# Attention on one core: the products of probabilities and values written as rows, instead of as columns that are copied and turned back

## The chip, the cores and the metric

The kernel runs on one core of a Trainium2 chip. TensorE (PE in the profile, PEld for its weight loads) does the matrix products, VectorE (DVE), ScalarE (ACT) and GpSimd (POOL) the rest; SyncE (SP) issues most transfers. The metric is the device time of one execution in microseconds (us), and less is better.

## What is computed

Two request groups, a prompt of 1024 tokens and a sample of 256, pass through two layers. Each layer has a mixer (an HGRN2 recurrence with 5 heads beside an attention with 6 heads in 3 groups) and a mixture of 16 experts. The change lies in the attention:

```python
def dilated_window_attention(q, k, v, dilation, radius):
    ...
    s = jnp.einsum('bnqhd,bnkhd->bnhqk', qs, kw)
    s = jnp.where(valid[None, :, None], s, -jnp.inf)
    m = jnp.max(s, axis=-1, keepdims=True)
    p = jnp.exp(s - m)
    l = jnp.sum(p, axis=-1, keepdims=True)
    o = jnp.einsum('bnqhk,bnkhd->bnqhd', p, vw) / jnp.transpose(l, (0, 1, 3, 2, 4))
    lse = jnp.transpose((m + jnp.log(l))[..., 0], (0, 1, 3, 2))
```

Windows and dilations are (128, 1), (512, 4) and (2048, 16), with two heads of 64 columns in each group. All of it is in fp32.

## The kernel before

Each layer runs in two parts. `mixers` holds the projections, the HGRN scan, the attention and the output projection; `moe` holds the experts. Within `mixers` the work is written as generators. `lanes` takes turns among them: each yields the number of nanoseconds that its next step should wait, and a clock that `mm`, `tr` and the wrapped engines advance by a modelled cost decides who records its next instructions. So the order of the instructions on each engine is fixed when the program is built, and a changed number of products or of yields in one generator moves the steps of the others as well.

The attention of a layer is cut into units of 128 queries and one head group (two heads): 24 units for the prompt and 6 for the sample, 60 over the two layers. A unit has one or two blocks of at most 128 keys; over both layers there are 96 blocks, so 192 products of probabilities and values (one for each block and head). Four of the units, at the two ends of the prompt in each layer, have one block of 64 keys. Up to three units are in flight, beside the HGRN lanes.

A unit's steps in `attention` are: load the rows; turn keys and queries (`kT`, `qT`); scores into PSUM (`sc`); mask and maximum on VectorE; exponentials on ScalarE; turn the probabilities (TensorE into a `tp` tile, ScalarE copies them to `PT`); multiply them with the values into another `tp` tile, `po`; bring the result to `ao` as rows (queries on partitions), and store it. `tp` is a PSUM pool of two buffers that the HGRN steps and the output projection share. `qT` is a pool of three buffers in SBUF, and before the change the copied result `oT` takes a buffer of it too: rows of the profile named `qT<-tp` are turned queries and copied results together, and TensorE rows `tp<-ident,qT` are the turns back.

In the profile a TensorE row such as `tp<-PT,kv 128*64 128x128` reads: written tile, moving operand, stationary operand; rows times columns of the stationary operand; shape of the moving operand. Each fp32 product leaves two records, one for each of its two passes with a weight load of its own; the products of fp32r operands (`mm<-hTh,wH` and the like, 512 columns wide) and the turns leave one. `lv<-Q,km 128*32` are small products of the HGRN scan, 32 columns and 32 rows of the array each, 16 in a group. Lines of helpers are L182 (`mm`), L196 (`tr`) and L111 (every operation of VectorE and ScalarE).

Of the kernel before, what the change touches and what calls it, by code (L numbers as in the profile page):

```python
# [8 lines left out]
F32 = mybir.dt.float32  # L9
# [3 lines left out]
AF = mybir.ActivationFunctionType  # L13
# [5 lines left out]
P = 128  # L19
# [106 lines left out]
class Body:  # L126
# [722 lines left out]
    def attention(self, groups, pool, width, scan):  # L849
        nc, I, sc_ps, tp = self.nc, self.I, self.scp, self.tpp  # L850
        am = pool.tile([P, 640], F32, name="am")
        nc.sync.dma_start(am, I["c_amask"])

        def rows_dma(g, dst, w0, nw, gi, spec):

            start, dims = spec
            base = g.qkv
            nsub = dims[0][1] if len(dims) == 2 else 1
            inner = dims[-1]
            for s in range(nsub):  # L860
                s0 = start + (s * dims[0][0] if len(dims) == 2 else 0)
                src = bass.AP(tensor=base.tensor, offset=base.offset + s0 * 9 * P + (3 * w0 + gi) * P,
                              ap=[[inner[0] * 9 * P, inner[1]], [3 * P, nw], [1, P]])
                nc.sync.dma_start(dst[s * inner[1]:(s + 1) * inner[1]], src)

        def transposed(src, name, bufs):
            n = src.shape[0]
            t = tp.tile([P, P], F32, name="tp")
            self.tr(t[:, :n], src)
            o = pool.tile([P, P], F32, name=name, bufs=bufs)  # L870
            nc.scalar.activation(o[:, :n], t[:, :n], AF.Copy)
            return o

        tiles = {}

        def unit(g, gi, qspec, kspec, m0):
            if kspec == "same":
                r = pool.tile([P, 3, P], F32, name="qkvr", bufs=3)
                rows_dma(g, r, 0, 3, gi, qspec)
                keys = [dict(n=P, k=r[:, 1], v=r[:, 2])]  # L880
            else:
                r = pool.tile([P, 1, P], F32, name="qr", bufs=3)
                rows_dma(g, r, 0, 1, gi, qspec)
                keys = []
                for name, k0, stride, n in kspec:
                    if name not in tiles:
                        kv = pool.tile([P, 2, P], F32, name="kv", bufs=5)
                        rows_dma(g, kv[:n], 1, 2, gi, (k0, [[stride, n]]))
                        tiles[name] = dict(n=n, k=kv[:n, 0], v=kv[:n, 1])
                    keys.append(tiles[name])  # L890
            yield 2500.0
            for k in keys:
                if "kT" not in k:
                    k["kT"] = transposed(k["k"], "kT", 5)
            qT = transposed(r[:, 0], "qT", 3)
            yield 150.0
            W = sum(k["n"] for k in keys)
            cuts, c = [], 0
            for k in keys:
                cuts.append((c, k["n"], k))  # L900
                c += k["n"]
            ps = [sc_ps.tile([P, W], F32, name="sc") for _ in range(2)]
            for c, n, k in cuts:
                for hd in range(2):
                    s = slice(64 * hd, 64 * hd + 64)
                    self.mm(ps[hd][:, c:c + n], qT[s, :], k["kT"][s, :n], start=True, stop=True)
            sc = pool.tile([P, 2, W], F32, name="sc", bufs=3)
            o = pool.tile([P, 132], F32, name="ao", bufs=3)
            nm = self.sm.tile([P, 2], F32, name="nm")
            for hd in range(2):  # L910
                nc.vector.tensor_tensor_reduce(sc[:, hd], ps[hd], am[:, m0:m0 + W], op0=OP.add, op1=OP.max,
                                               scale=1.0, scalar=NEG, accum_out=o[:, 128 + hd:129 + hd])
            nc.vector.tensor_scalar(nm, o[:, 128:130], -1.0, None, op0=OP.mult)
            self.after_all()
            for hd in range(2):
                nc.scalar.activation(sc[:, hd], sc[:, hd], AF.Exp, bias=nm[:, hd:hd + 1],
                                     accum_out=o[:, 130 + hd:131 + hd])
            yield 150.0
            pt = tp.tile([P, 2, len(keys), P], F32, name="tp")
            PT = pool.tile([P, 2, len(keys), P], F32, name="PT", bufs=3)  # L920
            for hd in range(2):
                for j, (c, n, k) in enumerate(cuts):
                    self.tr(pt[:n, hd, j], sc[:, hd, c:c + n])
            if all(n == P for c, n, k in cuts):
                nc.scalar.activation(PT, pt, AF.Copy)
            else:
                for j, (c, n, k) in enumerate(cuts):
                    nc.scalar.activation(PT[:n, :, j], pt[:n, :, j], AF.Copy)
            yield 150.0
            po = tp.tile([P, P], F32, name="tp")  # L930
            for j, (c, n, k) in enumerate(cuts):
                for hd in range(2):
                    s = slice(64 * hd, 64 * hd + 64)
                    self.mm(po[s], k["v"][:, s], PT[:n, hd, j], start=j == 0, stop=j == len(keys) - 1)
            oT = pool.tile([P, P], F32, name="qT", bufs=3)
            nc.scalar.activation(oT, po, AF.Copy)
            yield 150.0
            po = tp.tile([P, P], F32, name="tp")
            self.tr(po, oT)
            nc.vector.tensor_copy(o[:, 0:P], po)  # L940
            start, dims = qspec
            nsub = dims[0][1] if len(dims) == 2 else 1
            inner = dims[-1]
            for s in range(nsub):
                s0 = start + (s * dims[0][0] if len(dims) == 2 else 0)
                dst = bass.AP(tensor=g.ob.tensor, offset=g.ob.offset + (gi * g.nt + s0) * 132,
                              ap=[[inner[0] * 132, inner[1]], [1, 132]])
                nc.sync.dma_start(dst, o[s * inner[1]:(s + 1) * inner[1]])

        units = [(g,) + t for g in groups for t in self.attn_units(g)]  # L950

        def paced(i, u):
            yield from self.until(scan, "first", min(10, int(i * 0.4)))
            yield from unit(*u)
            scan[u[0].name] += 1

        tasks = [lambda i=i, u=u: paced(i, u) for i, u in enumerate(units)]
        yield from self.lanes(tasks, width)
# [509 lines left out]
```

## Time and profile before

| what | value |
| --- | --- |
| median of 3 runs | 3365.02 us (3363.21 to 3366.41) |
| the profiled execution | 3368.75 us, its span 3367.0 us |
| PE busy | 3251.8 us, 97% of the span, 23718 instructions |
| PEld busy | 2469.6 us, 73% |
| DVE busy | 2118.5 us, 63% |
| ACT busy | 1727.9 us, 51% |
| granted TensorE clock, mean | 0.984 |

The span runs from the first to the last instruction of the profiled execution; its own time has 1.75 us around that. Busy shares are averages over stages with different limits. The attention units stand from 365 to 726 us (layer 1) and from 2048 to 2407 us (layer 2), beside the HGRN scan and the first tiles of the output projection.

### The profile page before, as it was taken

To read this page: it belongs to the slowest core of one execution; us is meant where nothing else is said; L and a number is where in the kernel's file an instruction comes from. 1 tells how busy PE (TensorE), PEld (TensorE's weight loads), DVE (VectorE), ACT (ScalarE), POOL (GpSimd) and SP (SyncE) were. 2 spreads that over 40 slices of the span, in tenths; PEclk is the share of its full clock that TensorE was granted. 3 is DMA by queue.
4 is the path that set the end of the run, shared out by engine and by line. 5 is a ranking of instruction groups with operands and counts; after the bars stand their busy time and mean duration, and the time that the engine had idled before them with its cause. 6 is when DMAs were issued, how large, how long until landed. Compare 5 with 4: busy or idle time off the path is not lost.

```text
span 3367.0 us, 58960 instructions
## 1 busy us (share of the span) xinstructions
PE 3251.8 (97%) x23718; PEld 2469.6 (73%) x23718; DVE 2118.5 (63%) x4205; ACT 1727.9 (51%) x2509; POOL 248.9 (7%) x215
## 2 busy tenths in 40 slices
PE   8999999989799999999999999999997999999997
PEld 8999877767566666666699997777674666666664
DVE  6461377774756676666665615787746766676666
ACT  5331465552456666566553315555433666666665
POOL 0000000000011111011100000000000111111001
PEclk9999999999899999999999999999998999999999
DMA  5341221243498889888753412212434988889887
GB/s 186 109 134 51 87 63 52 75 136 124 162 319 284 285 284 332 287 280 283 240 167 99 129 52 83 62 57 76 139 126 158 330 314 285 284 288 327 284 283 282
DMA packets 421185, 639.52 MB, mean 190 GB/s; under 512 B 31024, under 2 KB 189360, under 8 KB 420912
## 3 DMA queue, kind: packets, MB, share of 16 engines
q1 hardware_dynamic: 396240, 556.83, 47.5%
q0 software_dynamic: 23952, 76.30, 8.3%
q8 instruction: 187, 3.06, 0.4%
q10 hardware_dynamic: 720, 2.62, 0.3%
q14 instruction: 86, 0.70, 0.1%
HBM read 550.09 MB, written 85.58 MB: 189 GB/s over the span
## 4 chain that ended last, share of the span: by engine, by line
PE 42%; DVE 3%; DMA 3%; ACT 1%; issue 1%; SPq 0%; DVEq 0%; ACTq 0%
PE mm L182 21%; PE lv L182 11%; PE sc L182 6%; PE tp L196 3%; PE tp L182 2%; DMA raw<-in_w_up_dram 1%; DVE wL L111 1%; DMA raw<-in_w_in_dram 0%; ACT wH L111 0%; DVE ind L111 0%; DVE val L111 0%; DMA obr<-obp 0%; DMA sg<-vgp 0%; DVE raw L111 0%; DMA xbp<-ye,idxp 0%
## 5 line engine op out<-in xcount | busy, mean ns | idle before, releaser
L111 DVE TENSOR_TENSOR wL<-raw,wH 128x2048 fp32r<-128x2048 f32 (+2 forms) x448 | 960.1, 2161 | 394.7 <-ACT wH L111 393.3
L111 ACT ACTIVATE wH<-raw 128x2048 fp32r<-128x2048 f32 (+2 forms) x448 | 812.4, 1816 | 255.2 <-PE lv L182 110.3
L182 PE MATMUL mm<-wH,hTh 128*128 128x320 f32 (+1 forms) x1120 | 367.0, 328 | 4.6 <-ACT wH L111 4.6
L182 PE MATMUL mm<-wL,hTh 128*128 128x320 f32 (+1 forms) x1120 | 360.6, 322 | 1.2 <-DVE wL L111 1.2
L182 PE MATMUL mm<-wH,hTl 128*128 128x320 f32 (+1 forms) x1120 | 360.8, 322 | 0.0
L182 PE MATMUL sc<-raw,xs 128*32 128x512 f32 x2048 | 231.0, 599 | 0.0
L182 PEld LDWEIGHTS mm<-wH,hTh 128*128 128x128 f32 x1120 | 211.8, 189 | 7.1 <-ACT wH L111 5.1
L182 PE MATMUL mm<-wH,xh 128*128 128x512 f32 x512 | 205.5, 401 | 8.9 <-ACT xh L111 8.9
L182 PEld LDWEIGHTS mm<-wL,hTh 128*128 128x128 f32 x1120 | 212.0, 189 | 2.2 <-DVE wL L111 1.9
L182 PEld LDWEIGHTS mm<-wH,hTl 128*128 128x128 f32 x1120 | 211.7, 189 | 0.7 <-DVE hTl L111 0.3
L182 PE MATMUL mm<-wL,xh 128*128 128x512 f32 x512 | 205.6, 402 | 3.6 <-DVE wL L111 3.6
L182 PE MATMUL lv<-wL,xh 128*128 128x512 f32 x512 | 200.6, 392 | 3.5 <-DVE wL L111 3.5
L182 PE MATMUL mm<-hTh,wH 128*128 128x512 f32 x480 | 202.8, 423 | 0.0
L182 PE MATMUL mm<-wH,xl 128*128 128x512 f32 x512 | 201.8, 394 | 0.0
L182 PE MATMUL lv<-wH,xl 128*128 128x512 f32 x512 | 200.2, 391 | 0.0
L182 PE MATMUL lv<-wH,xh 128*128 128x512 f32 x512 | 200.1, 391 | 0.0
L182 PE MATMUL mm<-hTl,wH 128*128 128x512 f32 x480 | 195.8, 408 | 0.0
L182 PE MATMUL mm<-hTh,wL 128*128 128x512 f32 x480 | 194.0, 404 | 0.0
L1317 POOL DMA_INDIRECT xbs<-yS,sidx x62 | 95.3, 1537 | 1111.7 <-ACT yS L111 980.3
L182 PEld LDWEIGHTS sc<-raw,xs 128*32 128x32 f32 x2048 | 63.9, 111 | 148.2 <-issue 146.0
L182 PE MATMUL sc<-raw,hs 128*32 128x512 f32 x1024 | 150.6, 598 | 0.0
L111 DVE TENSOR_TENSOR K<-K,TT 128x256 f32<-128x256 f32 (+1 forms) x360 | 123.9, 374 | 39.1 <-PE lv L182 27.9
(305 smaller groups left out, 6315.2 us busy)
## 6 DMA issues: line engine op xcount, KB each, us to landing
raw<-in_w_up_dram SPq DMA_DIRECT2D x128, 1024.0 KB, 15.7
raw<-in_w_down_dram SPq DMA_DIRECT2D x128, 1024.0 KB, 8.9
raw<-in_w_gate_dram SPq DMA_DIRECT2D x126, 1024.0 KB, 14.0
raw<-in_w_in_dram SPq DMA_DIRECT2D x36, 512.0 KB, 4.2
wr<-in_w_in_dram SPq DMA_DIRECT2D x24, 512.0 KB, 3.8
raw<-in_w_in_dram SPq DMA_DIRECT2D x16, 640.0 KB, 4.6
vgp<-vgo SPq DMA_DIRECT2D x64, 160.0 KB, 1.8
raw<-in_w_in_dram SPq DMA_DIRECT2D x12, 768.0 KB, 4.7
```

Source lines behind the costliest of these rows:

```text
L111: return fn(out, *args, **kw)
L182: self.last_mm = self.nc.tensor.matmul(out, lhsT, rhs, start=start, stop=stop)
L196: ins = self.nc.tensor.transpose(out, src, self.ident[:k, :k])
L1317: nc.gpsimd.indirect_dma_start(out=xs2, out_offset=at, in_=yS[64 * h:64 * h + 64], in_offset=None, compute_op=OP.add)
```

## The change

The product of probabilities and values changes its roles. Before, the values are stationary (128 keys by 64 columns of one head) and the turned probabilities move (128 queries); the result has the head's columns on partitions, the two heads on the two halves of the partitions. ScalarE copies it, TensorE turns it, and VectorE copies it to `ao`. After, the turned probabilities are stationary (128 keys by 128 queries) and the head's 64 value columns move; the result has queries on partitions already, and VectorE copies it to `ao` at once. The copy, one wait of the generator (`yield 150.0`), one `tp` tile and the turn fall away. The loop over heads now stands outside the loop over key blocks.

```diff
             po = tp.tile([P, P], F32, name="tp")
-            for j, (c, n, k) in enumerate(cuts):
-                for hd in range(2):
-                    s = slice(64 * hd, 64 * hd + 64)
-                    self.mm(po[s], k["v"][:, s], PT[:n, hd, j], start=j == 0, stop=j == len(keys) - 1)
-            oT = pool.tile([P, P], F32, name="qT", bufs=3)
-            nc.scalar.activation(oT, po, AF.Copy)
-            yield 150.0
-            po = tp.tile([P, P], F32, name="tp")
-            self.tr(po, oT)
+            for hd in range(2):
+                s = slice(64 * hd, 64 * hd + 64)
+                for j, (c, n, k) in enumerate(cuts):
+                    self.mm(po[:, s], PT[:n, hd, j], k["v"][:, s], start=j == 0, stop=j == len(keys) - 1)
             nc.vector.tensor_copy(o[:, 0:P], po)
```

How the order moves is shown at three places. The first is on TensorE in layer 1, beside the level products of an HGRN unit (`lv<-Q,km`), where three attention units end close together; a row here is one product, written tile, moving and stationary operand, shape of the output.

```order
-L182 MATMUL tp<-PT,kv 64x128 x8
-L196 MATMUL tp<-ident,qT 128x128
-L182 MATMUL lv<-Q,km 32x32 x8
-L196 MATMUL tp<-ident,qT 128x128
-L182 MATMUL lv<-Q,km 32x32 x3
-L196 MATMUL tp<-ident,qT 128x128
-L182 MATMUL lv<-Q,km 32x32 x5
+L182 MATMUL tp<-kv,PT 128x64 x4
+L182 MATMUL mm<-hTh,wH 128x512
+L182 MATMUL mm<-hTl,wH 128x512
+L182 MATMUL mm<-hTh,wL 128x512
+L182 MATMUL mm<-hTh,wH 128x512
+L182 MATMUL tp<-kv,PT 128x64 x4
+L182 MATMUL mm<-hTl,wH 128x512
+L182 MATMUL mm<-hTh,wL 128x512
+L182 MATMUL lv<-Q,km 32x32 x16
```

Three turns that cut the group of 16 small products into pieces are gone, and the units' products now stand among the 512-column products, apart from each other.

The second place is further on in layer 1, on TensorE, where a pair of units stands among the projection's products only.

```order
 L182 MATMUL mm<-hTh,wH 128x512
-L182 MATMUL tp<-PT,kv 64x128 x8
-L196 MATMUL tp<-ident,qT 128x128
-L182 MATMUL mm<-hTl,wH 128x512
-L182 MATMUL mm<-hTh,wL 128x512
-L196 MATMUL tp<-ident,qT 128x128
+L182 MATMUL tp<-kv,PT 128x64 x8
+L182 MATMUL mm<-hTl,wH 128x512
+L182 MATMUL mm<-hTh,wL 128x512
 L182 MATMUL mm<-hTh,wH 128x512
 L182 MATMUL mm<-hTl,wH 128x512
```

The eight products stand at the same place in either order; the two turns behind them fall away, and nothing takes their place.

The third is on VectorE, early in layer 1: the copies into `ao` among the steps of an HGRN level (`K`, `Q`, `ac`).

```order
+L111 COPY ao<-tp 128x128
 L111 COPY_PREDICATED ac<-cmask,lv 128x128
 L111 TENSOR_TENSOR Q<-Q,TT 128x32x2x8
+L111 COPY ao<-tp 128x128
 L111 TENSOR_TENSOR qk<-qk,mm 128x512
-L111 TENSOR_TENSOR K<-K,TT 128x16x16 x2
-L111 COPY ao<-tp 128x128 x3
+L111 TENSOR_TENSOR K<-K,TT 128x16x16
+L111 COPY ao<-tp 128x128
+L111 TENSOR_TENSOR K<-K,TT 128x16x16
```

Three copies that stood together behind a level's steps now stand one by one, two of them ahead of that level's steps.

## Rows read from the trace of the kernel before

**Rows 1.** Busy time of each engine in two stretches (us, instructions).
```profile
core 0: us, PE busy (x) PEld busy (x) DVE busy (x) ACT busy (x) POOL busy (x), PEclk, DMA share, GB/s
360.00:660.00 300.00, 298.29 (x3433) 229.16 (x3433) 208.25 (x633) 173.91 (x389) 4.52 (x6) 1.00 0.23 67
...
2300.00:2405.00 105.00, 98.10 (x1068) 73.75 (x1068) 82.95 (x289) 62.68 (x154) 3.49 (x5) 0.93 0.31 90
```

**Rows 2.** The tile PT: TensorE records, duration ns min/median/max, first and last start, forms.
```profile
L182 PE MATMUL tp<-PT,kv x288: 269/273/476, 378.9 to 2377.9; 128*64 128x128 f32 x136, 64*64 64x128 f32 x8
...
L182 PE MATMUL tp<-PT,qkvr x96: 272/273/473, 568.0 to 2397.8; 128*64 128x128 f32 x96
```

**Rows 3.** The tile qT, the same view.
```profile
L111 ACT ACTIVATE qT<-tp x120: 258/277/297, 371.1 to 2398.2; 128x128 f32<-128x128 f32 x120
...
L196 PE MATMUL tp<-ident,qT x60: 270/327/421, 381.7 to 2399.6; 128*128 128x128 f32 x60
```

**Rows 4.** TensorE's timeline: start us, us, merged records; sixteen records in one group.
```profile
501.91 1.09 PE L182 MATMUL tp<-PT,kv 128*64 128x128 f32 x16
```

**Rows 5.** TensorE's timeline, weight loads, around the router's products on 16 columns.
```profile
783.14 0.30 PEld L182 LDWEIGHTS sc<-quad,xT 128*128 128x128 f32 x2
...
783.36 0.19 PEld L182 LDWEIGHTS mm<-oL,wH 128*128 128x128 f32 x1
```

**Rows 6.** TensorE's timeline: HGRN products with 128 stationary columns, back to back.
```profile
2404.85 0.39 PE L182 MATMUL tp<-v,A 128*128 128x128 f32 x2
2405.07 0.61 PE L182 MATMUL tp<-S,Q 128*128 128x128 f32 x4
2405.52 0.39 PE L182 MATMUL tp<-v,A 128*128 128x128 f32 x2
```

**Rows 7.** Timelines of TensorE's products and of its weight loads: a score on 64 moving columns.
```profile
371.41 0.43 PE L182 MATMUL sc<-kT,qT 64*128 64x64 f32 x2
...
371.41 0.29 PEld L182 LDWEIGHTS sc<-kT,qT 64*128 64x128 f32 x2 [0.39 <-ACT qT L111]
```

**Rows 8.** TensorE's timeline: a turn back among 512-column products.
```profile
381.26 0.39 PE L182 MATMUL mm<-hTh,wL 128*128 128x512 f32 x1
381.49 0.39 PE L182 MATMUL mm<-hTh,wH 128*128 128x512 f32 x1
381.72 0.27 PE L196 MATMUL tp<-ident,qT 128*128 128x128 f32 x1
381.75 0.47 PE L182 MATMUL mm<-hTl,wH 128*128 128x512 f32 x1
382.06 0.39 PE L182 MATMUL mm<-hTh,wL 128*128 128x512 f32 x1
```

**Rows 9.** TensorE's timeline: turns back among the small products.
```profile
435.40 0.33 PE L196 MATMUL tp<-ident,qT 128*128 128x128 f32 x1
435.66 0.26 PE L182 MATMUL lv<-Q,km 128*32 128x32 f32 x6
435.85 0.33 PE L196 MATMUL tp<-ident,qT 128*128 128x128 f32 x1
436.11 0.31 PE L182 MATMUL lv<-Q,km 128*32 128x32 f32 x10
```

**Rows 10.** TensorE's timeline: a unit's eight records among 512-column products.
```profile
537.14 0.40 PE L182 MATMUL mm<-hTh,wL 128*128 128x512 f32 x1
537.47 0.66 PE L182 MATMUL tp<-PT,kv 128*64 128x128 f32 x8
538.06 0.50 PE L182 MATMUL mm<-hTh,wH 128*128 128x512 f32 x1
```

**Rows 11.** TensorE's waits: us in total, times, longest.
```profile
PEld tp L196 <- ACT qT L111: 4.1, 18, 0.3
```

**Rows 12.** The tile ao: VectorE's copies, and the engine's idle time ahead of them (us, times).
```profile
L111 DVE COPY ao<-tp x60: 278/291/292, 382.0 to 2400.0; 128x128 f32<-128x128 f32 x60
...
  PE tp L196: 35.2, 44
```

**Rows 13.** Busy times, as in Rows 1, near the end of layer 2's scan.
```profile
2357.00:2367.00 10.00, 8.61 (x130) 7.11 (x131) 8.82 (x22) 7.76 (x15) 0.00 (x0) 0.66 0.41 122
```

## Prediction

> **What bounds the kernel.** I read the busy times by stretch first, because the attention stands in two stretches only. In the 300 us of layer 1 in which most units run, TensorE is busy for 298.3 us at full clock, VectorE for 208 and ScalarE for 174 [rows 1]. So in that stretch TensorE's own occupation is the time, and a step of another engine costs nothing unless TensorE waits for it. Only the seams behind the scans are different: in the 105 us from 2300 us TensorE idles for 6.9 us and its mean granted clock is 0.93 [rows 1]. The rest of the reading is therefore a count of TensorE's occupation: how many passes, how many turns, and what it costs to change how the array is divided.
>
> Durations in the timeline overlap (a record of 0.27 us is followed by the next after 0.11), so I price by the distance from one start or end to the next, never by durations.
>
> **The passes.** The tile PT has 288 and 96 records, 384 in all [rows 2]: 192 products, two passes each. Before, the two heads of a block run side by side on the two halves of the array's columns. The group of sixteen records lasts 1.09 us; without its last record's 0.273 us [rows 2] it is 0.82 us for seven steps of two records each, 0.117, in which the first weight load still counts [rows 4]. I take 0.11 for a step of both heads: 384 / 2 x 0.11 = 21.1 us before.
>
> After, the stationary operand has 128 columns and takes the whole array, so the heads follow one another: 384 steps. No row shows a whole-array fp32 product with 64 moving columns, so I bound it. Fp32 products with 128 stationary and 128 moving columns run at (2405.52 - 2404.85) / 6 = 0.112 us a pass [rows 6]. Halving the moving columns helps only if the weight load keeps up. With 16 moving columns, two loads take 0.30 us where one takes 0.19, so they start 0.11 apart, and the next load starts at 0.22 [rows 5]: the load of 128 fp32 columns is the limit, whatever moves. The score on 64 moving columns agrees: its second load ends 0.29 after the first starts, again 0.11 apart [rows 7]. So 0.11 a pass: 384 x 0.11 = 42.2 us, **21.1 us more** than before. The lower bound is what the 64 columns need when weights cost nothing: the second record of that score starts 0.43 - 0.27 = 0.16 after the first, and 0.16 - 0.106 = 0.054 is left for moving [rows 7]; 384 x 0.054 = 20.7, 0.4 less than before. The upper bound is that load and move add up, 0.16: 61.4, 40.3 more.
>
> **The turns.** Among 512-column products a start follows the last after 0.23 us, and 0.57 where a turn stands between two steps [rows 8]: 0.57 - 0.46 = 0.11 a turn. Sixty turns [rows 3]: **6.6 us less**.
>
> **The divisions.** From one turn to the next, with six small products between them, are 0.45 us; ten small products last 0.05 longer than six, so six take some 0.07, and the turn costs 0.38, of which 0.27 is neither the turn nor the products [rows 9]: the array goes over to another division and back. A unit's eight records between 512-column products: from the end of one product to the end of the next 538.56 - 537.54 = 1.02, less that product's own 0.23 [rows 8] and four steps of 0.11, leaves 0.35 for the two changes [rows 10]. So a change costs 0.14 to 0.18; I take 0.16, since groups of both kinds fall away. Counted over TensorE's whole order, with four divisions (whole, column halves, row halves of the scores, small), there are 1008 changes before and 919 after. In this the units with a 64-key block are worse off: the loop over heads now goes between 64 and 128 rows four times a unit, once before. 89 x 0.16 = **14.2 us less** (12 at 0.14, 16 at 0.18).
>
> Here a rule speaks against the change. The Trainium skill, TensorEngine Tiling (Array Packing), section "When to Use Tiling", advises for at most 64 moving columns the opposite step: swap stationary and moving, and tile the columns for up to twice the speed. The trace agrees on the steps (both heads in 0.11) but shows the 0.27 to 0.35 us around each group beside it. By that rule alone the sum would lack the divisions and come to 12.5 us more; by the rows it is the sum below.
>
> **What goes from ScalarE, and what waits.** `qT<-tp` has 120 records of 0.277 us [rows 3], and 60 of them are the copied results: 16.6 us less on an engine that has 126 of 300 us free [rows 1], so by itself nothing. The turns' weight loads waited for that copy for up to 4.1 us [rows 11]. Part of that lies under the change of division; I take half, **2 us less**. VectorE's copy into `ao` stays, 60 of 0.29 [rows 12]. It now waits for the unit's products themselves. Queued behind it are the level steps (`ac`, `K`, `Q`) that the next small products need. They have cover: VectorE is free for 92 of 300 us [rows 1].
>
> **Sum:** +21.1 - 6.6 - 14.2 - 2 = -1.7 us. Against the profiled execution's 3368.75 us that is 3367.0; the median of the runs is 3.7 us lower, so 3363.3 there. With the passes at their bounds the sum is -23.2 or +17.5. So I forecast no difference that can be told: three terms of 15 to 21 us that nearly cancel. About 0.2% (6.7 us) is what a measurement of this kernel can tell from no change.
>
> **Rivals.**
>
> *The seams gain.* Behind layer 2's scan the clock is 0.66 on average in 10 us with 1.4 us of idle [rows 13], so part of that time ran at 1.2 instead of 2.4 GHz; the 105 us lose 6.9 us to idle time and some 7 to the clock [rows 1]. The sample's units end there. With ScalarE relieved and two steps fewer in each unit, half of this could go: 7 us more, 3356. Against it: the order there still has the same HGRN turns and products, waiting for the same copies. Chance 0.19.
>
> *The load is hidden.* Passes at 0.054: 3365.0 - 23.2 = 3342. For it only that a 64-column move is short; against it [rows 5, 7]. Chance 0.05.
>
> *VectorE's queue (slower).* The copy into `ao` stands directly behind the products, and VectorE already stood idle ahead of it for 35.2 us in 44 cases [rows 12]. A two-block unit's eight passes take 0.88 us where the turn took 0.11, so 60 copies could hold the queue for 0.77 x 60 = 46 us more at most, ahead of level steps. If a third reaches TensorE through late `K` and `km`, 15 us: 3378. It decides from 8.4 us on, a fifth. For it speaks that two of three copies moved ahead of their level's steps; against it, VectorE's free third. Chance 0.08.
>
> *Load and move add up (slower).* 0.16 a pass, +17.5: 3382. The score's second record, 0.16 after the first, speaks for it; but it followed a first load that nothing could hide [rows 7], and loads in a row are 0.11 apart [rows 5]. Chance 0.07.
>
> *The divisions give nothing back (slower).* If the 0.16 is not the change itself but a pause that the next product would have anyway, the sum is +21.1 - 6.6 - 2 = +12.5: 3377. Against it: a turn among 512-column products costs its bare 0.11 [rows 8], and 0.38 among small ones [rows 9]. Chance 0.06. It is the time that the section on tiling leads to.
>
> **How the numbers follow.** The forecast has 0.55. Within it: the steps at 0.109 or 0.112, a change at 0.14 or 0.18 and the waits at 0 or 4 move it by some 2 us each, and the new order shifts the seams by a few us either way, so 3358 to 3371. Faster: the seams and the hidden load, 0.24. Same: 0.55. Slower: 0.08 + 0.07 + 0.06 = 0.21. The range from 3348 to 3378 leaves out the hidden load, the added load and an edge of the others, some 0.17.
>
> **What would show it.** Right: records `tp<-kv,PT` with 128 stationary columns, 384 of them with those of `qkvr`, at 0.11 from start to start; no gap of 0.2 to 0.3 us before and after a group among 512-column products; the small products in whole groups of 16; 60 records of `qT<-tp` instead of 120; TensorE's busy time in the two stretches within a few us. Wrong: passes at 0.06 or 0.16; VectorE's idle time ahead of `ao` well over 35 us with new waits of TensorE for `km` or `K`; a seam with more or less low clock than before. The sum is a difference of large terms, so an error of a tenth in the step alone (2 us) changes its sign, and the seams alone can make the kernel faster or slower by more than the sum.

## The result, and the profile after

The changed kernel takes 3384.36 us (median of 6 runs, 3380.55 to 3385.93), the kernel before 3365.72 beside it (6 runs, 3356.63 to 3368.08): a ratio of 1.0053 [1.0043, 1.0062]. It is 18.6 us slower, where 3363 was forecast and the range ended at 3378.

The page of the changed kernel's profile, whose own time is 3385.93 us:

```profile
span 3384.1 us, 58779 instructions
...
PE 3264.9 (96%) x23658; PEld 2498.3 (74%) x23658; DVE 2118.1 (63%) x4205; ACT 1711.7 (51%) x2447; POOL 250.1 (7%) x215
```

TensorE has 60 instructions less and is busy 13.1 us longer. The two stretches of [rows 1], in the same view:

```profile
360.00:660.00 300.00, 296.44 (x3388) 233.81 (x3387) 205.85 (x628) 166.29 (x361) 4.52 (x6) 1.00 0.23 66
2300.00:2405.00 105.00, 96.87 (x1026) 73.33 (x1025) 77.52 (x268) 53.83 (x130) 3.48 (x5) 0.84 0.26 76
```

Within the scan little moved: 296.44 us busy for 298.29, at full clock. At the end of layer 2's scan the granted clock is 0.84 where it was 0.93. That is the first hint.

The tiles PT and qT, which answer [rows 2] and [rows 3]:

```profile
L182 PE MATMUL tp<-kv,PT x288: 217/275/476, 379.7 to 2387.1; 128*128 128x64 f32 x136, 64*128 64x64 f32 x8
L182 PE MATMUL tp<-qkvr,PT x96: 217/275/476, 569.5 to 2408.9; 128*128 128x64 f32 x96
...
L111 ACT ACTIVATE qT<-tp x60: 252/276/290, 371.9 to 2404.1; 128x128 f32<-128x128 f32 x60
```

There are 384 whole-array passes with 64 moving columns, and 60 copies by ScalarE instead of 120. TensorE's timeline gives their price (the place answers [rows 10]):

```profile
540.84 0.48 PE L182 MATMUL mm<-hTh,wH 128*128 128x512 f32 x1
541.15 1.00 PE L182 MATMUL tp<-kv,PT 128*128 128x64 f32 x8
541.96 0.48 PE L182 MATMUL mm<-hTl,wH 128*128 128x512 f32 x1
```

From the end of one 512-column product (541.32) to the end of the next (542.44) are 1.12 us; less that product's own 0.23 [rows 8], 0.89 is left for eight passes: 0.111 each, and nothing for a change of division. Before, the same unit took 0.79 there [rows 10] and a turn behind it. So the passes cost what was forecast.

The idle time of VectorE ahead of its copy into `ao`, which answers [rows 12]:

```profile
its engine sat idle before it (us, times) until:
  PE tp L182: 56.6, 48
```

It is 56.6 us in 48 cases, before 35.2 in 44.

So where are 17.2 us (the two profiled executions, 3385.93 - 3368.75)? I cut each layer at three records of TensorE: the first and the last projection product (`mm<-hTh` or `mm<-hTl`) bound the **scan**; from there to the first router product (`sc<-xT,wr`) is the **seam**. Layer 1's scan goes from 361.0 to 679.6 before and from 361.9 to 682.9 after; its seam ends at 743.5 and 749.4. Layer 2's scan goes from 2034.2 to 2353.6 and from 2038.5 to 2358.3; its seam ends at 2419.2 and 2434.0. The scans grow by 2.4 + 0.4 = 2.8 us, the seams by 2.6 + 10.1 = **12.7 us**; all the rest gives 1.7. The seam of layer 2 after, busy times in pieces of 5 us (the columns of [rows 1]; the clock is the third number from the end):

```profile
2373.30:2378.30 5.00, 4.42 (x49) 2.94 (x49) 3.47 (x15) 2.52 (x8) 0.00 (x0) 0.79 0.37 124
2378.30:2383.30 5.00, 5.00 (x16) 2.91 (x16) 2.89 (x22) 2.34 (x10) 0.00 (x0) 0.50 0.00 0
2383.30:2388.30 5.00, 3.57 (x46) 2.99 (x46) 3.23 (x12) 3.57 (x10) 0.00 (x0) 0.50 0.50 135
2388.30:2393.30 5.00, 4.63 (x45) 3.35 (x46) 3.01 (x10) 0.42 (x2) 0.00 (x0) 0.50 0.15 40
2393.30:2398.30 5.00, 4.20 (x42) 2.37 (x42) 3.43 (x14) 2.23 (x8) 0.00 (x0) 0.50 0.26 68
2398.30:2403.30 5.00, 4.84 (x15) 4.19 (x16) 3.97 (x9) 0.70 (x2) 0.65 (x2) 0.50 0.42 132
2403.30:2408.30 5.00, 5.00 (x30) 3.86 (x28) 3.45 (x13) 3.91 (x12) 1.33 (x2) 0.98 0.73 239
```

The same place in the kernel before:

```profile
2373.60:2378.60 5.00, 4.99 (x23) 3.38 (x23) 4.21 (x14) 3.35 (x13) 0.00 (x0) 0.50 0.49 135
2378.60:2383.60 5.00, 4.31 (x111) 2.82 (x109) 4.26 (x14) 2.42 (x6) 0.00 (x0) 0.94 0.43 129
2383.60:2388.60 5.00, 4.59 (x35) 3.43 (x32) 4.87 (x15) 2.37 (x6) 0.00 (x0) 1.00 0.23 59
```

Both fall to 0.50 (1.2 GHz) near here. Before, the clock is back at 2.4 GHz after 6.8 us, at 2379.2; after, it stays low for 27.3 us, to 2403.5, though TensorE is busy for 71 to 100% of each piece.

### The profile page after: what moved, and what is told of

Same layout as the page of the kernel before. It is cut to its first block, busy times and chain, and to the rows that moved or that the text cites. A ratio compares the mean times of both kernels' runs of the same rounds, so it can differ in the third digit from the quotient of the medians.

```text
span 3384.1 us, 58779 instructions
## 1 busy us (share of the span) xinstructions
PE 3264.9 (96%) x23658; PEld 2498.3 (74%) x23658; DVE 2118.1 (63%) x4205; ACT 1711.7 (51%) x2447; POOL 250.1 (7%) x215
## 4 chain that ended last, share of the span: by engine, by line
PE 42%; DVE 3%; DMA 3%; ACT 1%; issue 1%; SPq 0%; DVEq 0%; ACTq 0%
PE mm L182 21%; PE lv L182 11%; PE sc L182 6%; PE tp L196 3%; PE tp L182 2%; DMA raw<-in_w_up_dram 1%; DMA raw<-in_w_in_dram 1%; DVE wL L111 1%; ACT wH L111 0%; DVE ind L111 0%; DVE val L111 0%; DMA obr<-obp 0%; DVE raw L111 0%; DMA or<-in_w_out_dram 0%; DMA xbp<-ye,idxp 0%
## 6 DMA issues: line engine op xcount, KB each, us to landing
raw<-in_w_up_dram SPq DMA_DIRECT2D x128, 1024.0 KB, 17.2
```

## The experiments

Two theories were set against each other, both about the seams. **Form**: the new products, with 64 moving columns, keep the clock low where they stand. **Order**: the new costs move the steps of other generators, and the seam gets worse waits. Beside them stood the rivals of the prediction that add time everywhere.

The table has all kernels: the median (us) and the ratio to the kernel before, which ran with each set of them (3365.84 beside the first four experiments, 3366.19 beside wide, sample_timed and sample_counted, 3367.18 beside sample_wide, order_kept and order_only, 3366.17 beside the last two); and from the one profiled execution of each its own time, the scans and seams (layer 1 / layer 2, us), and the stretches at 1.2 GHz that begin between the scan's end and 20 us behind the seam, counted whole. The last column is of all executions of a kernel: the mean of twice the span times what the execution's mean granted clock lacks of 1, which is its whole time at 1.2 GHz (the means are sure to 1 to 5 us, one standard error; by the profiles 73 to 89 us of it lie outside the seams in every kernel).

| kernel | median, ratio | profiled | scans | seams | at 1.2 GHz | all runs, 1.2 GHz |
| --- | --- | --- | --- | --- | --- | --- |
| before | 3365.72 | 3368.75 | 318.6 / 319.4 | 63.9 / 65.6 | 10.2 / 13.6 | 99 |
| after | 3384.36, 1.0053 | 3385.93 | 321.0 / 319.8 | 66.5 / 75.7 | 23.9 / 40.9 | 141 |
| sample_old | 3371.83, 1.0015 | 3371.38 | 320.5 / 322.8 | 62.1 / 66.1 | 10.2 / 20.4 | 111 |
| prompt_old | 3373.7, 1.0020 | 3377.17 | 319.0 / 318.7 | 67.1 / 70.5 | 23.8 / 34.1 | 116 |
| after_early | 3365.99, 0.9997 | 3365.51 | 330.3 / 333.6 | 51.5 / 51.8 | 13.6 / 13.6 | 95 |
| before_early | 3361.38, 0.9982 | 3362.12 | 332.7 / 326.2 | 50.9 / 50.9 | 10.2 / 6.8 | 96 |
| wide | 3377.38, 1.0032 | 3380.74 | 321.4 / 322.9 | 65.1 / 70.2 | 10.2 / 27.2 | 111 |
| sample_timed | 3370.91, 1.0012 | 3376.39 | 319.3 / 319.6 | 63.6 / 70.3 | 13.6 / 37.5 | 115 |
| sample_counted | 3369.68, 1.0007 | 3371.21 | 320.6 / 319.4 | 65.2 / 63.1 | 17.0 / 13.6 | 105 |
| sample_wide | 3371.61, 1.0017 | 3371.61 | 319.1 / 318.5 | 65.6 / 66.2 | 13.6 / 17.0 | 104 |
| order_kept | 3370.16, 1.0008 | 3375.87 | 321.5 / 319.2 | 63.4 / 68.9 | 10.2 / 34.1 | 110 |
| order_only | 3371.89, 1.0017 | 3372.31 | 318.3 / 322.1 | 63.6 / 69.9 | 13.6 / 23.9 | 108 |
| yield_kept | 3377.36, 1.0038 | 3377.26 | 322.6 / 319.2 | 62.7 / 74.7 | 10.2 / 37.5 | 130 |
| count_kept | 3379.89, 1.0041 | 3384.97 | 321.3 / 319.8 | 66.0 / 74.6 | 23.9 / 37.5 | 134 |

Over all runs the changed kernel spends 42 us more at 1.2 GHz than the kernel before. If TensorE lost half of them, that would be 21 us (an estimate), as much as the whole loss of 18.6; so the low clock is no accident of the profiled executions.

**sample_old and prompt_old.** One group's units in the new form, the other's with the products, copy, wait and turn of before. In sample_old the test is for "s".

```diff
+            if g.name == "p":
+                po = tp.tile([P, P], F32, name="tp")
+                for j, (c, n, k) in enumerate(cuts):
...
+                self.tr(po, oT)
+            else:
+                po = tp.tile([P, P], F32, name="tp")
+                for hd in range(2):
...
```

> Prompt units in the new form, sample units in the old one (copy and turn back). On TensorE the order up to the end of the scans is that of the changed kernel, the seam behind layer 2's scan nearly that of the kernel before. Seam theory: the 18 us lie in the seams behind the two scans, where the sample's units end and TensorE stays at 1.2 GHz for 65 us instead of 24; with the old sample units most of it goes, 3364 to 3371 us, and the low clock in the seams falls below 35 us. Pass theory: the doubled passes and VectorE's waits in the scans cost it; 3380 to 3385 us, with the scans 8 us longer each.

> The reverse: prompt units in the old form, sample units in the new one. The order up to the end of both scans is exactly that of the kernel before. Seam theory: 3376 to 3385 us, the scans as before (318.6 and 319.4 us), the seams 2 to 10 us longer with 45 us or more of low clock. Pass theory: 3365 to 3369 us, since only 24 of the 192 products have the new form.

Measured: 1.0015 [1.0006, 1.0024] with the prompt's 160 products changed, 1.0020 [1.0011, 1.0030] with the sample's 32, by the medians 6.0 and 7.9 us (beside 3365.84). Both lie between the two theories' times, nearer to the seam theory's. The sample has a sixth of the products and costs about as much as all the others. A price for each pass can't do that, so the rivals on the pass and on the divisions fall. Five of the sample's six units in each layer stand in the seams, 48 of its 64 passes, and the prompt's units all stand in the scans. The profiles place the two costs accordingly: in sample_old the scans are 5.3 us longer than before and the seams 1.3 shorter, in prompt_old the seams are 8.1 us longer and the scans 0.3 shorter. Together the two medians make 13.9 us, 4.7 short of 18.6; with some 3 us either way on each, that does not tell whether they act apart from each other.

**after_early and before_early.** Units are admitted earlier, so that they end within the scan; the seams then hold no attention products.

```diff
-            yield from self.until(scan, "first", min(10, int(i * 0.4)))
+            yield from self.until(scan, "first", min(10, int(i * 0.3)))
```

> The changed kernel with its attention units started earlier: unit i waits for 0.3 i instead of 0.4 i of the ten steps of the scan, so that no unit's products stand behind the end of the scan. Seam theory: without sample units the seams hold output products and the last HGRN turns only, so the low clock there falls to 20 us or less and the time to 3355 to 3368 us. Pass theory: the passes stay as they are, 3380 us or more.

> The kernel before with the same earlier start, as the partner of the run after_early. Seam theory: the seams are alike in both, and the two differ by the sum of the scans alone, within 5 us of each other; 3355 to 3368 us. Pass theory: this one is 15 us or more faster than after_early.

Measured: 0.9997 [0.9988, 1.0006] and 0.9982 [0.9973, 0.9990]. With no units in the seams the two forms are 3365.99 - 3361.38 = 4.6 us apart instead of 18.6, and the seams are equal within 1 us. So some 14 of the 18.6 us need the units in the seams. Both medians came out as the seam theory had them. The old form, admitted earlier, is 4.5 us below the kernel before and 23 below the changed one.

**wide.** The changed kernel, but each product moves all 128 value columns and half of its result is not used.

```diff
-            po = tp.tile([P, P], F32, name="tp")
+            po = tp.tile([P, 2, P], F32, name="tp")
...
-                    self.mm(po[:, s], PT[:n, hd, j], k["v"][:, s], start=j == 0, stop=j == len(keys) - 1)
+                    self.mm(po[:, hd], PT[:n, hd, j], k["v"], start=j == 0, stop=j == len(keys) - 1)
```

> The changed kernel, but each product moves the 128 value columns of both heads instead of the head's own 64, and VectorE copies the two halves that count. Half of what TensorE computes there is thrown away. If the load of 128 weights sets the pace, a pass stays at 0.112 us and the scans as long as in the changed kernel (321.0 and 319.8 us, within 3); if the 64 columns set it, the 384 passes take 20 us more. For the seams: if the clock stays low because passes with 64 moving columns keep the array half empty, the low clock in the seams falls from 65 to below 35 us and the time to 3366 to 3374 us; if it stays low because of where the sample's units stand in the seam (the order), it stays at 45 us or more and the time at 3378 to 3388.

(VectorE's copy then takes the two halves that count.) Measured: 1.0032 [1.0021, 1.0044], 7.0 us less than the changed kernel though twice as much moves. Its tile PT has the shape, and a pass still costs 0.112 in place (0.90 for the eight at 2110.15 us):

```profile
L182 PE MATMUL tp<-kv,PT x288: 270/276/583, 380.6 to 2386.1; 128*128 128x128 f32 x136, 64*128 64x128 f32 x8
```

Twice the moving columns make a pass no longer, so the move does not set it; the load of the 128 weight columns, 0.11 us apart in [rows 5], does. The Trainium skill, TensorE: Matmul & The Clock Gate, section "LDWEIGHTS (loading the stationary operand)", says that a load's time goes with the stationary operand's columns. The traces agree so far: with 128 columns in both kernels a pass takes 0.111 and 0.112 us; no run here loads fewer in a whole-array pass.

The median and the low clock of the profile (37.4 us) lie between what the two theories said. Over all runs the time at 1.2 GHz falls by 30 us, from 141 to 111, and the kernel gets only 7.0 us faster; what the wider moves cost elsewhere is not parted. The order moved a little too, so the 7 us alone don't tell form from order.

**sample_timed and sample_counted.** Two attempts to move the order alone, in the sample's units. sample_timed is prompt_old with the sample's new products, and steps in place of copy, wait and turn, advancing the program's clock as the old ones did; sample_counted is the kernel before, whose clock counts the sample's products as long as the new ones (`P / 0.6 + 4` in place of `P / 2.4` below).

```diff
+                        t0 = self.clock
                         self.mm(po[:, s], PT[:n, hd, j], k["v"][:, s], start=j == 0, stop=j == len(keys) - 1)
+                        self.clock = t0 + P / 2.4
+                        self.dep = self.end = self.clock + 100.0
```

> As prompt_old (prompt units old, sample units new), but the recording clock is moved on in the sample units as the old form would have moved it, its wait of 150 ns included, so the seam's order comes closer to that of the kernel before (0.85 to 0.89 of it alike instead of 0.81 to 0.85). If the form of the 32 products in the seams costs the time, it stays at 3372 to 3376 us, as prompt_old; if the order does, it falls to 3364 to 3370 us and the low clock in the seams from 58 to below 40 us.

> The kernel before in all its instructions; only the recording clock counts each product of probabilities and values of the sample's units at 217 ns instead of 53, which moves a few products in the seams (0.91 and 0.97 of the order alike), and nothing before the end of a scan. If the order in the seam alone can move the clock, the time moves by 4 us or more either way and the low clock with it; if the form is needed, it stays at 3363 to 3368 us with 20 to 28 us of low clock.

Measured: 1.0012 [1.0002, 1.0021] and 1.0007 [0.9998, 1.0016]. Both lie between what the theories said: inconclusive. In sample_timed's profile the low clock, 51.1 us, lies with the form.

**sample_wide.** prompt_old with 128 moving columns in the sample's products (half of the result not used, as in wide). From the end of layer 2's scan to well behind the first units in its seam TensorE's order is the same, but for one turn that stands two passes earlier.

```diff
-                po = tp.tile([P, P], F32, name="tp")
+                po = tp.tile([P, 2, P], F32, name="tp")
...
-                        self.mm(po[:, s], PT[:n, hd, j], k["v"][:, s], start=j == 0, stop=j == len(keys) - 1)
+                        self.mm(po[:, hd], PT[:n, hd, j], k["v"], start=j == 0, stop=j == len(keys) - 1)
```

> The prompt's units in the old form, the sample's 32 products in the new form but with 128 moving value columns each, of which half of the result is thrown away. TensorE's order is almost that of the kernel with only the sample's units changed, and no pass gets cheaper, since a pass of 128 columns took 0.11 us as well. If it is what the products leave idle in the array that keeps the clock low in the seams, the doubled columns give most of the 8 us back: 3366 to 3369 us, low clock in the seams back to about 10 and 20 us. If it is only the order, nothing changes: 3372 to 3375 us, low clock about 24 and 34 us. If wider moves cost time by themselves: over 3376.

Measured: 1.0017 [1.0007, 1.0027] in total, not to be told from prompt_old's 1.0020; the total decides nothing. The place does. TensorE's timeline of prompt_old in layer 2's seam (start us, us; the last bracket is idle time and its releaser):

```profile
2379.25 0.48 PE L196 MATMUL tp<-ident,sc 128*128 128x128 f32 x1 [0.15 <-ACT sc L111]
2379.52 1.38 PE L182 MATMUL tp<-kv,PT 128*128 128x64 f32 x6
2380.70 0.42 PE L196 MATMUL tp<-ident,sc 128*128 128x128 f32 x1
2380.91 0.53 PE L182 MATMUL tp<-kv,PT 128*128 128x64 f32 x2
2381.37 0.66 PE L182 MATMUL lv<-Q,km 128*32 128x32 f32 x32
2381.95 1.12 PE L182 MATMUL tp<-qkvr,PT 128*128 128x64 f32 x4
2382.83 0.77 PE L182 MATMUL mm<-oL,wH 128*128 128x512 f32 x1
...
2388.28 0.80 PE L182 MATMUL sc<-kT,qT 64*128 64x128 f32 x4
```

The same of sample_wide:

```profile
2375.92 0.47 PE L196 MATMUL tp<-ident,sc 128*128 128x128 f32 x1 [0.15 <-ACT sc L111]
2376.18 1.06 PE L182 MATMUL tp<-kv,PT 128*128 128x128 f32 x4
2377.04 0.42 PE L196 MATMUL tp<-ident,sc 128*128 128x128 f32 x1
2377.25 0.82 PE L182 MATMUL tp<-kv,PT 128*128 128x128 f32 x4
2378.00 0.46 PE L182 MATMUL lv<-Q,km 128*32 128x32 f32 x32
2378.39 0.71 PE L182 MATMUL tp<-qkvr,PT 128*128 128x128 f32 x4
2378.86 0.48 PE L182 MATMUL mm<-oL,wH 128*128 128x512 f32 x1
...
2382.37 0.49 PE L182 MATMUL sc<-kT,qT 64*128 64x128 f32 x4
```

From the turn to the scores `sc<-kT,qT` are 9.03 us with 64 moving columns and 6.45 with 128. The small products behind the first unit take 0.66 and 0.46: the clock rose among the wide products. The windows of the two show when, prompt_old first:

```profile
2373.80:2394.30 20.50, 19.39 (x185) 14.43 (x184) 14.29 (x54) 9.03 (x29) 0.00 (x0) 0.50 0.33 91
2394.30:2414.30 20.00, 19.38 (x125) 16.22 (x124) 14.58 (x53) 9.19 (x24) 1.99 (x3) 1.00 0.35 108
```

```profile
2370.90:2377.70 6.80, 6.65 (x46) 5.26 (x39) 5.41 (x23) 4.28 (x17) 0.00 (x0) 0.50 0.40 102
2377.70:2398.20 20.50, 16.53 (x180) 11.95 (x180) 16.54 (x55) 10.52 (x30) 1.98 (x3) 1.00 0.51 156
```

1.2 GHz lasts 20.5 us with 64 moving columns, 6.8 us with 128. Two more kernels repeat prompt_old's side: order_kept and sample_timed have its order on TensorE, and its 64 columns, for the first 278 products of this seam, to 11 us behind the fall of the clock. Their windows, order_kept first:

```profile
2373.90:2394.40 20.50, 20.34 (x186) 15.46 (x186) 14.78 (x52) 8.87 (x26) 0.00 (x0) 0.50 0.36 104
```

```profile
2369.70:2390.20 20.50, 20.35 (x186) 15.40 (x177) 14.94 (x50) 8.69 (x26) 0.00 (x0) 0.50 0.36 102
```

So in this place it is the form, three executions against one. Over all runs the time at 1.2 GHz is 104 us for sample_wide and 116 for prompt_old, 12 us less with a standard error of 5, which agrees. Two things stay in doubt. An earlier stretch at 1.2 GHz in this seam, ahead of these products and in the same order, lasts 3.4 us in sample_wide and 6.8 in the other three, so the executions differ by more than these products. And the medians show no time gained with the clock.

**order_kept and order_only.** The two theories crossed for all units. order_kept has the new products, but the program's clock goes on as with the old products, copy, wait and turn; order_only has the instructions of before, with the new products' cost in the program's clock.

The core of order_kept, behind each product and behind the loops:

```diff
+                    self.clock = t0 + P / 2.4
+                    self.dep = self.end = self.clock + 100.0
+            act = nc.scalar
+            act.free = max(act.free, self.dep) + act.least + act.per_elem * P
+            self.end = max(self.end, act.free)
+            yield 150.0
+            self.clock += 112.0
+            self.dep = self.end = self.clock + 100.0
```

And of order_only:

```diff
+                    self.clock = t0 + P / 0.6 + 4
+                    self.dep = self.end = self.clock + 100.0
```

> All units in the new form, but the clock by which the program sets its order is advanced as by the old products, copy and turn, so that TensorE's order lies nearer to that of before. If the order that the new costs bring is what lengthens the seams, most of the 18.5 us goes: 3368 to 3374 us, with low clock near the 10 and 14 us of before. If it is the form of the products wherever they stand: 3380 to 3386, low clock 24 and 40 us.

> The instructions of the kernel before, all value products counted by the program's clock as long as the new ones, so that only the order moves. If the order is the cause: 3374 to 3382 us, with low clock of 20 to 40 us in the seams. If the form is: 3362 to 3369 us, low clock 10 to 20 us.

Measured: 1.0008 [0.9999, 1.0017] and 1.0017 [1.0007, 1.0027]. By the totals the order is needed: the new form in an order nearer to the old one costs 3.0 us beside its kernel before (3367.18). But the order with the old form costs only 4.7, less than forecast for it, so it isn't the order alone either. In order_kept's profile the low clock of layer 2's seam is still 34.1 us; that execution took 5.7 us more than the kernel's median, so its seams may be longer than in most. Over all runs the time at 1.2 GHz is 11 us above the kernel before in order_kept and 9 in order_only, beside 42 with both. VectorE's idle time ahead of `ao` in order_kept:

```profile
its engine sat idle before it (us, times) until:
  PE tp L182: 54.6, 45
```

This wait is almost that of the changed kernel, without its loss. So it isn't what costs the 18.6 us.

**yield_kept and count_kept.** Parts of order_kept: the changed kernel with the wait alone (below), and with the first two lines of order_kept alone.

```diff
+            yield 150.0
             nc.vector.tensor_copy(o[:, 0:P], po)
```

> The changed kernel with the wait of 150 ns kept between a unit's products and VectorE's copy. TensorE's order is that of the changed kernel to the end of both scans and differs only in the seams, by about a tenth of the rows. If VectorE's copy, recorded directly behind the products, holds up VectorE's queue, most of the loss goes: 3368 to 3374 us, and VectorE's idle time ahead of that copy falls well below 56.6 us. If it is the order in the seams, the time moves through the seams alone, either way: 3372 to 3390 us with scans of 320 to 321 us. If it is the new form of the products: 3382 to 3387 us.

> The changed kernel with its value products advancing the program's clock as the old ones did, and nothing else. TensorE's order is the same as with the kept wait, except in the seam of layer 2, where a few rows in a hundred differ. If the order in the seams decides, the scans stay at 320 to 321 us, the first seam equals that of the kernel with the kept wait within 1 us, and the total lies between 3370 and 3388 us as the low clock in the seams goes. If it is the new form: 3382 to 3387 us.

Measured: 1.0038 [1.0024, 1.0052] and 1.0041 [1.0027, 1.0055], 7.0 and 4.5 us below the changed kernel's 3384.36. Both medians lie where the order theory had them, below what the form alone should cost. VectorE's idle time ahead of `ao` in yield_kept is 55.2 us, not well below 56.6, and most of the loss stays, so the theory that its copy holds up VectorE's queue falls. Layer 2's seam stays at 74.7 and 74.6 us with 37.5 at 1.2 GHz in both. The seam of layer 1 has one and the same order on TensorE in the two, and yet 62.7 us with 10.2 at 1.2 GHz, and 66.0 with 23.9. I had expected them equal within 1 us. The changed kernel has this order too up to the 341st of the seam's 502 products: the longest stretch at 1.2 GHz that begins before that lasts 13.7 us there, 6.8 in yield_kept and 17.1 in count_kept. So one order gives different lengths from one execution to the next, and a difference of some 10 us at 1.2 GHz between two single profiles shows nothing by itself.

## Why the prediction was wrong

- **Passes, +21.1: right at full clock.** 384 passes at 0.111 us. That load and move add up, or that the load is hidden, both fell: a pass costs the same with 64 and with 128 moving columns.
- **Turns and divisions, -6.6 and -14.2: right in place.** The turns are gone, a group of eight passes stands among 512-column products without a gap, and its 0.89 us beside 0.79 and a turn is what the terms say. The count of changes was a little high: over TensorE's records in the two traces, in the same four divisions, I find 1022 and 941, so 81 fewer and 13.0 us. The rival that the divisions give nothing back fell with it: its 12.5 us would have to appear in the scans, in proportion to the products, and the scans grew by 2.8 us.
- **Waits, -2: wrong in sign, by a little.** The sum for all units was -1.7 us. The scans gave +2.8, in sample_old +5.3, and the pair without units in the seams +4.6. So 4 to 7 us were missed. Which wait they are is open: VectorE waits 21 us longer ahead of `ao`, but order_kept shows that wait without the loss, and no run parts the rest.
- **The seams: the step that failed.** "The new order shifts the seams by a few us either way": they took 12.7 us, three quarters of the loss. The rival *the seams gain* had the place and the quantity (low clock) and the wrong sign. It counted what leaves ScalarE, and not how long the clock stays low around the new passes. In layer 2's seam the units stand in a stretch at 1.2 GHz; with the old products, two heads side by side with 128 moving columns, 2.4 GHz was back after 6.8 us, with the new ones after 27.3. The sum also priced every pass at 2.4 GHz. That matters less: in prompt_old's lines twelve passes take 1.18 + 0.46 + 0.88 us, 0.21 each, and in the kernel before four steps took 0.91 (the last two lines below), so the 16 new passes within the 27.3 us cost some 1.5 us more than 8 old steps (an estimate), of the seam's 10.1.
- **How sure that is.** In layer 2's seam it was shown at one place in one order (sample_wide beside prompt_old, order_kept and sample_timed). Over the kernels that admit units as before, the six with 64 moving columns in the sample's units have 34.1 to 40.9 us at 1.2 GHz there and seams of 68.9 to 75.7; the other six 13.6 to 27.2, and 63.1 to 70.2. The means are 72.5 and 66.9, so the form is worth some 5.6 us of the 10.1 in this seam (an estimate, since the orders differ within both sixes). In layer 1's seam the same two sixes have 64.9 and 64.3 us: there the form shows no cost. Of the rest in layer 2, one wait of TensorE is plain, and it goes with the order. Its timeline in the changed kernel:

```profile
2382.82 1.11 PE L196 MATMUL tp<-ident,sc 128*128 128x128 f32 x4
2385.36 0.47 PE L196 MATMUL tp<-ident,sc 128*128 128x128 f32 x1 [1.43 <-ACT sc L111]
2385.63 1.38 PE L182 MATMUL tp<-kv,PT 128*128 128x64 f32 x6
```

  And the kernel before at the same step:

```profile
2374.07 1.11 PE L196 MATMUL tp<-ident,sc 128*128 128x128 f32 x4
2375.20 0.79 PE L182 MATMUL mm<-oL,wH 128*128 128x512 f32 x1
2375.79 0.63 PE L182 MATMUL mm<-oH,wL 128*128 128x512 f32 x1
2376.22 0.63 PE L182 MATMUL mm<-oH,wH 128*128 128x512 f32 x1
2376.64 0.63 PE L196 MATMUL tp<-ident,sc 128*128 128x128 f32 x2
2377.20 1.12 PE L182 MATMUL tp<-PT,kv 128*64 128x128 f32 x8
2378.11 0.64 PE L182 MATMUL tp<-PT,qkvr 128*64 128x128 f32 x4
```

  Three products of the output projection bridged the wait for ScalarE's exponentials; in the new order they stand ahead of it, and TensorE waits for 1.43 us. yield_kept has the same wait and the long seam; order_kept and prompt_old have the bridge, and shorter seams.
- **Open.** How the loss divides between form and order in total: both together cost 18.6 us, the order with the old form 4.7, the form near the old order 3.0. They don't add up, as if one made the other worse. Why the clock stays low around the new products is not shown, and neither is why the length differs between executions of one TensorE order in layer 1's seam.

## What to carry to other kernels

Count an edit's passes in the stretch where TensorE is busy at full clock, but price the stretches with a falling clock apart: there products of one price per pass went with 1.2 GHz for 20.5 or for 6.8 us, and a sixth of the products, most of them in the seams, cost about as much as all the rest. Before trusting "a few us either way" for an order that moves, list which units stand in the seams and what bridges each wait there. Where single profiles of one order differ, take the granted clock of all runs beside them. If work can be moved out of a seam altogether, try that first: here it took 18.4 us off the changed kernel and 4.5 off the kernel before.

## What the runs showed of the hardware

- The granted clock stayed at 1.2 GHz for 27.3 us while TensorE was busy for 24.54 of them (90%), in the changed kernel's seam from 2376.2 to 2403.5 us; I had taken a busy TensorE to be at 2.4 GHz. In sample_wide's seam, which differs from prompt_old's there in the place of one turn and in 128 instead of 64 moving columns of one kind of product, it stayed there for 6.8 instead of 20.5 us. In order_kept and sample_timed TensorE was busy for 20.34 and 20.35 of 20.5 us and the clock stayed at 1.2 GHz all the while.
- A whole-array fp32 pass with 128 stationary columns costs 0.111 us with 64 moving columns and 0.112 with 128.
- At 1.2 GHz such a pass costs 0.21 us with 64 moving columns (2.52 for twelve in prompt_old) and 0.22 with 128 (0.86 for four in sample_wide).
- Eight whole-array passes between 512-column products cost nothing beside themselves (0.89 us), while a unit in the old form lost 0.35 us there to its two changes of division [rows 10].
